# Hybrid S5 and differential-attention layer: the low-k pass of the scores as two matmuls on 64 rows

## The chip, the cores and the metric

The kernel runs on one core of one Trainium2 chip. The metric is device time in microseconds (us), the median of several executions. One further execution was taken by the hardware profiler; the rows below come from it.

## The reference, cut to what matters

One encoder layer is applied to two requests, a prompt of 256 tokens and a sample of 1024 tokens. Beside the attention it has a state-space branch, gates and projections, which the change leaves alone. The part in question:

```python
q = _rotary(q.reshape(Bsz, L, N_HEADS, 2, HEAD_DIM))   # 4 heads, 2 streams, 64 channels
k = _rotary(k.reshape(Bsz, L, N_HEADS, 2, HEAD_DIM))
def block(qi):                                         # 128 queries at a time
    s = jnp.einsum('bqhtd,bkhtd->bthqk', qi, k).astype(jnp.float32) * scale
    p = jax.nn.softmax(s, axis=-1)
    w = p[:, 0] - lam * p[:, 1]
    return jnp.einsum('bhqk,bkhe->bqhe', w, v)
```

## The kernel before, in words

The kernel works at float32 accuracy with a faster matmul type: every operand is split into a high part and a low part (suffixes h and l), and a product is the sum of high·high, high·low and low·high.

The attention stage goes head by head (4 heads). A head has five pairs of query blocks: four pairs over the 1024 sample tokens (pi 0 to 3, the long units) and one over the 256 prompt tokens (pi 4, the short units). A unit is one block of 128 queries (qi). `unit_scores` computes, for each of the two streams t, a score tile S of 128 queries by nk keys (two banks of 512 float32 columns for a long unit). Its contraction has only 64 channels, so q's tile holds the high part in partitions 0 to 63 and the low part in 64 to 127, and the k tile holds the same 64 channels twice. One matmul on 128 rows with k's high part (line 924) thus gives high·high plus low·high. A second one with k's low part (line 926) gives high·low plus low·low. For each t of a long unit that is four matmuls of 512 columns: two at line 924, two at line 926.

Behind the scores VectorE (DVE) takes the row maximum (line 928), ScalarE (ACT) the exponential (line 932), GpSimd (POOL) and VectorE combine the two streams (lines 939, 940). TensorE (PE) transposes the weights (line 949) and multiplies them with v (lines 961 to 963). Between these stand "filler" steps (lines 706 to 708), gate projections that are independent of the attention and are interleaved by counts (`F_LONG`, `F_SHORT`). A static scheduler fixes each engine's order when the program is built.

`load_head` loads a head's operands from DRAM on SyncE's (SP's) DMA queue into buffers shared with the earlier stage. In the rows the tags are: hU (q of t=0, and v's high part), htb (k's high part of t=0, and q of t=1), hmt (k's low part of t=0, and v's low part), hwcm (k's high part of t=1, and the short units' parts), hwb (k's low part of t=1). All tags have two buffers, hwb has one.

Two other places of the program use only a part of the array and are read below: line 440, in the preparation of the state-space matrices, with 32 columns of the array (shape "128*32"), and lines 275 and 276 with 32 of its rows ("32*128").

Of the kernel before, what the change touches and what calls it, by code (L numbers as in the profile page):

```python
# [11 lines left out]
F32 = mybir.dt.float32  # L12
# [10 lines left out]
LL = 1024  # L23
LS = 256
NT = LL + LS
# [101 lines left out]
def kernel(  # L127
# [6 lines left out]
    V, G, A, PE, SP = nc.vector, nc.gpsimd, nc.scalar, nc.tensor, nc.sync  # L134
# [3 lines left out]
    def dram(shape, dtype, name):  # L138
        return tc.dram_tile(shape, dtype, name=name)
# [7 lines left out]
    q_d = [dram([2, 2, 128, NT], F32, f"q_d{i}") for i in range(2)]  # L147
    k_d = [dram([2, 2, 128, NT], F32, f"k_d{i}") for i in range(2)]
# [572 lines left out]
    def fill(steps, ins=None):  # L721
        with after(ins):
            for _ in range(steps):
                next(filler, None)
# [4 lines left out]
    with ExitStack() as p2:  # L729
# [20 lines left out]
        def load_wb(b):  # L750
            wb = (sp_ if b % 2 else sl).tile([128, 2, NB, 128], F32, tag="wb", name="wb")
            SP.dma_start(wb, wb_d[b])
            return wb
# [81 lines left out]
        with tc.manual_schedule(engines={mybir.EngineType.PE, mybir.EngineType.SP}):  # L835
# [10 lines left out]
            for b in range(NBLK):  # L846
                q = b // 2
# [22 lines left out]
    with ExitStack() as p3:  # L870
# [5 lines left out]
        def load_head(h):  # L876
            pr, cb = h // 2, (h % 2) * 2
            big = lambda tag, b: sl.tile([128, NT], F32R, tag=tag, name=f"h{tag}", bufs=b)
            sml = lambda tag, b: sl.tile([128, LL], F32R, tag=tag, name=f"h{tag}", bufs=b)
            q0, k00, q1, vh = big("U", 2), big("tb", 2), big("tb", 2), big("U", 2)  # L880
            k10, k01, k11, vl, rest = sml("mt", 2), sml("wcm", 2), sml("wb", 1), sml("mt", 2), sml("wcm", 2)
            part = lambda i: rest[:, i * LS:(i + 1) * LS]
            v3 = lambda t: t.rearrange("p (k e) -> p k e", e=128)

            def load_q(t, q):
                rows = slice((cb + t) * 32, (cb + t) * 32 + 32)
                for s in range(2):
                    for f in range(2):
                        o = s * 64 + f * 32
                        SP.dma_start(q[o:o + 32].bitcast(F32), q_d[pr][s, f, rows])  # L890

            def load_k(t, hl, k, c0, n):
                rows = slice((cb + t) * 32, (cb + t) * 32 + 32)
                for s in range(2):
                    for f in range(2):
                        o = s * 64 + f * 32
                        SP.dma_start(k[o:o + 32].bitcast(F32), k_d[pr][hl, f, rows, c0:c0 + n])

            load_q(0, q0)
            load_k(0, 0, k00, 0, NT)  # L900
            load_k(0, 1, k10, 0, LL)
            load_q(1, q1)
            load_k(1, 0, k01, 0, LL)
            load_k(1, 1, k11, 0, LL)
            SP.dma_start(v3(vh).bitcast(F32), vh_d[h])
            SP.dma_start(v3(vl).bitcast(F32), vl_d[h][:, 0:8])
            load_k(0, 1, part(0), LL, LS)
            load_k(1, 0, part(1), LL, LS)
            load_k(1, 1, part(2), LL, LS)
            SP.dma_start(v3(part(3)).bitcast(F32), vl_d[h][:, 8:10])  # L910
            return (([q0[:, :LL], q1[:, :LL]], [k00[:, :LL], k01], [k10, k11], v3(vh)[:, 0:8], v3(vl)),
                    ([q0[:, LL:], q1[:, LL:]], [k00[:, LL:], part(1)], [part(0), part(2)],
                     v3(vh)[:, 8:10], v3(part(3))))

        def unit_scores(hd, qi, nk, fu):
            qs, kh, kl = hd[:3]
            pt = []
            sm = ap.tile([128, 2], F32, tag="sm", name="sm", bufs=2)
            for t in range(2):
                S = ps_s.tile([128, LL], F32, tag=f"S{t}", name=f"S{t}")  # L920
                qw = qs[t][:, qi * 128:qi * 128 + 128]
                cks = [(c, min(512, nk - c)) for c in range(0, nk, 512)]
                for c, n in cks:
                    PE.matmul(S[:, c:c + n], qw, kh[t][:, c:c + n], start=True, stop=False)  # L924
                for c, n in cks:
                    last = PE.matmul(S[:, c:c + n], qw, kl[t][:, c:c + n], start=False, stop=True)  # L926
                mx = ap.tile([128, 1], F32, tag=f"mx{t}", name=f"mx{t}", bufs=2)
                V.tensor_reduce(mx, S[:, :nk], axis=AX.X, op=ALU.max)  # L928
                V.tensor_scalar(mx, mx, -1.0 / math.sqrt(HD), None, op0=ALU.mult)  # L929
                p = ap.tile([128, LL], F32, tag=f"p{t}", name=f"p{t}", bufs=3 - t)  # L930
                with tc.issue_after(tables.ins):
                    A.activation(p[:, :nk], S[:, :nk], AF.Exp, bias=mx, scale=1.0 / math.sqrt(HD),  # L932
                                 accum_out=sm[:, t:t + 1])
                pt.append(p)
                fill(fu[t], last if fu[t] else None)
            rs = ap.tile([128, 2], F32, tag="rs", name="rs", bufs=2)
            V.reciprocal(rs, sm)  # L937
            V.tensor_tensor(rs[:, 1:2], rs[:, 1:2], nlam, op=ALU.mult)
            G.tensor_scalar(pt[0][:, :nk], pt[0][:, :nk], rs[:, 0:1], 1.0, op0=ALU.mult, op1=ALU.mult)  # L939
            V.scalar_tensor_tensor(pt[0][:, :nk], pt[1][:, :nk], rs[:, 1:2], pt[0][:, :nk], op0=ALU.mult, op1=ALU.add)  # L940
            return pt[0]
# [71 lines left out]
        for h in range(NH):  # L1013
            parts = load_head(h)
            for pi in range(5):
                nk = LL if pi < 4 else LS
                fl = F_LONG if pi < 4 else F_SHORT
                hd = parts[pi // 4]
                wTh = ap.tile([128, 8, 256], F32R, tag="wTh", name="wTh", bufs=2)
                wTl = ap.tile([128, 8, 256], F32R, tag="wTl", name="wTl", bufs=2)  # L1020
                for qi in range(2):
                    w = unit_scores(hd, (pi % 4) * 2 + qi, nk, fl)
                    if prev:
                        finish(prev, fl[2])
                    else:
                        fill(fl[2])
                    fill(fl[3])
                    prev = (h, pi, qi, w, hd, wTh, wTl)
# [21 lines left out]
    def split_into(h, l, src):  # L1050
        ins = A.copy(h, src)
        V.tensor_tensor(l, src, h, op=ALU.subtract)
        return ins
# [98 lines left out]
    for grp in range(2):  # L1152
# [4 lines left out]
        wb = load_wb(0)  # L1157
        for f in range(8):
            bh, bl = wb
            if f < 7:  # L1160
                wb = load_wb(f + 1)
# [13 lines left out]
            last = split_into(mh[:, f], ml[:, f], s1)  # L1175
# [75 lines left out]
```

## Time and profile before

| | us |
|---|---|
| median of 3 runs | 1127.63 (1127.1 to 1129.29) |
| the profiled execution's own time | 1127.2 |
| its span | 1125.1 |
| TensorE busy (matmul) | 1067.2 |
| TensorE busy (weight load) | 987.1 |
| VectorE busy | 801.0 |
| ScalarE busy | 462.5 |
| GpSimd busy | 354.8 |

The span is the time from the first to the last recorded instruction. "PE" is the matmul row of TensorE, "PEld" its weight loads, which overlap the matmuls. Matmuls are pipelined: one is recorded longer than the distance to the next, so that distances between starts say what a stream of them costs. A row of the timeline may merge neighbours of one line ("x2"); its time then runs from the first one's start to the last one's end.

### The profile page before, as it was taken

How to read it: one execution, taken by the hardware profiler on the slowest of the kernel's cores; microseconds unless marked ns; L12 is line 12 of the kernel's file. 1: busy time of each engine (PE TensorE's matmuls, PEld its weight loads, DVE VectorE, ACT ScalarE, POOL GpSimd, SP SyncE). 2: the span in 40 equal slices, each digit the busy share in tenths (PEclk: the TensorE clock that was granted, in tenths of full speed). 3: DMA queues.
4: the chain of work that ended last, by engine and by line, in shares of the span. 5: the costliest groups of instructions: out<-in, count | busy, mean ns of one | idle time of the engine just before them, and what ended most of it. 6: DMA issues, size and time to landing. Idle time of an engine off the chain costs nothing.

```text
span 1125.1 us, 18000 instructions
## 1 busy us (share of the span) xinstructions
PE 1067.2 (95%) x6479; PEld 987.1 (88%) x6479; DVE 801.0 (71%) x1533; ACT 462.5 (41%) x927; POOL 354.8 (32%) x437
## 2 busy tenths in 40 slices
PE   5999799999989999999999999999999999998997
PEld 4878588788979988898999998989999999998997
DVE  5998997888579999478677777766442675666524
ACT  4453222332312121455555645554453445544332
POOL 2447999511032333122122222212141003520032
PEclk9999899999999999999999999999999999999999
DMA  7745453654596676615416316311645975569112
GB/s 212 170 141 188 142 174 117 209 166 156 173 282 174 205 202 168 177 51 150 141 47 169 122 47 186 114 40 60 210 124 174 292 230 128 167 194 270 48 57 94
DMA packets 186154, 173.59 MB, mean 154 GB/s; under 512 B 32721, under 2 KB 161745, under 8 KB 186066
## 3 DMA queue, kind: packets, MB, share of 16 engines
q1 hardware_dynamic: 150738, 144.13, 43.6%
q10 hardware_dynamic: 35328, 28.32, 7.9%
q8 instruction: 51, 0.84, 0.3%
q14 instruction: 37, 0.30, 0.1%
HBM read 113.71 MB, written 58.69 MB: 153 GB/s over the span
## 4 chain that ended last, share of the span: by engine, by line
PE 47%; DVE 18%; DMA 7%; ACT 4%; issue 3%; POOL 2%; SPq 0%; ACTq 0%; POOLq 0%; DVEq 0%
PE mm L706 5%; PE mm L707 5%; PE mm L708 5%; PE xb L1058 3%; PE xb L1059 3%; PE xb L1060 3%; PE pb L246 2%; PE pb L248 2%; PE pb L247 2%; DVE z L797 2%; DVE z L798 2%; PE S L924 2%; DMA yt<-ya_d 2%; PE S L926 2%; DVE mx L928 2%
## 5 line engine op out<-in xcount | busy, mean ns | idle before, releaser
L706 PE MATMUL mm<-hTh,wh 128*128 128x424 f32 (+1 forms) x576 | 212.2, 368 | 6.3 <-ACT zo L712 6.3
L708 PE MATMUL mm<-hTh,wl 128*128 128x424 f32 (+1 forms) x576 | 206.1, 358 | 0.0
L707 PE MATMUL mm<-hTl,wh 128*128 128x424 f32 (+1 forms) x576 | 206.0, 358 | 0.0
L706 PEld LDWEIGHTS mm<-hTh,wh 128*128 128x128 f32 x576 | 109.2, 190 | 12.6 <-ACT zo L712 8.1
L707 PEld LDWEIGHTS mm<-hTl,wh 128*128 128x128 f32 x576 | 109.2, 190 | 4.6
L708 PEld LDWEIGHTS mm<-hTh,wl 128*128 128x128 f32 x576 | 109.0, 189 | 3.4
L928 DVE TENSOR_REDUCE mx<-S 128x1 f32<-128x1024 f32 (+1 forms) x80 | 84.2, 1057 | 38.9 <-PE S L926 38.7
L939 POOL TENSOR_SCALAR p<-p,rs 128x1024 f32<-128x1024 f32 (+1 forms) x40 | 41.7, 1042 | 205.0 <-DVE rs L937 194.2
L246 PE MATMUL pb<-hTh,wh 128*128 128x512 f32 (+1 forms) x288 | 105.7, 367 | 0.0
L247 PE MATMUL pb<-hTl,wh 128*128 128x512 f32 (+1 forms) x288 | 105.1, 365 | 0.0
L932 ACT ACTIVATE p<-S,mx 128x1024 f32<-128x1024 f32 (+1 forms) x80 | 79.2, 992 | 63.0 <-DVE mx L929 53.8
L248 PE MATMUL pb<-hTh,wl 128*128 128x512 f32 (+1 forms) x288 | 103.9, 361 | 0.4 <-DVE wl L240 0.4
L240 POOL TENSOR_TENSOR wl<-wst,wh 128x1024 fp32r<-128x1024 f32 x24 | 64.3, 2679 | 126.5 <-ACT wh L239 51.7
L1191 PE MATMUL tr<-wqh,mh 128*128 128x256 f32 x320 | 89.7, 280 | 1.5 <-DVE o L1195 1.3
L1192 PE MATMUL tr<-wql,mh 128*128 128x256 f32 x320 | 89.3, 279 | 0.0
L1193 PE MATMUL tr<-wqh,ml 128*128 128x256 f32 x320 | 89.0, 279 | 0.0
L248 PEld LDWEIGHTS pb<-hTh,wl 128*128 128x128 f32 x288 | 54.6, 190 | 9.3 <-DVE wl L240 0.9
L246 PEld LDWEIGHTS pb<-hTh,wh 128*128 128x128 f32 x288 | 54.7, 190 | 8.6
L1191 PEld LDWEIGHTS tr<-wqh,mh 128*128 128x128 f32 x320 | 60.1, 188 | 2.4 <-DVE o L1195 2.4
L247 PEld LDWEIGHTS pb<-hTl,wh 128*128 128x128 f32 x288 | 54.6, 190 | 8.4
L1198 POOL TENSOR_TENSOR o<-o,finB 128x256 f32<-128x256 f32 x30 | 27.9, 934 | 103.8 <-ACT jk L1197 103.8
L1192 PEld LDWEIGHTS tr<-wql,mh 128*128 128x128 f32 x320 | 60.1, 188 | 0.0
(387 smaller groups left out, 2793.4 us busy)
## 6 DMA issues: line engine op xcount, KB each, us to landing
wst<-in_w_in_dram ACTq DMA_DIRECT2D x24, 512.0 KB, 4.0
wst<-in_w_in_dram SPq DMA_DIRECT2D x16, 512.0 KB, 4.8
wst<-in_w_branch_dram SPq DMA_DIRECT2D x32, 256.0 KB, 4.4
wqs<-in_w_out_dram SPq DMA_DIRECT2D x16, 512.0 KB, 3.8
tt_d<-tt SPq DMA_DIRECT2D x16, 320.0 KB, 2.6
tb<-tt_d SPq DMA_DIRECT2D x8, 640.0 KB, 5.1
zt<-gs_d SPq DMA_DIRECT2D x16, 320.0 KB, 4.3
x<-in_x_sample_dram SPq DMA_DIRECT2D x8, 512.0 KB, 4.6
```

Of the source, the lines that this page charges most:

```text
L240: e.tensor_tensor(lv, st, hv, op=ALU.subtract)
L246: PE.matmul(ps[:, :n], wh[:, k, :], hTh[:, k, c0:c0 + n], start=(k == 0), stop=False)
L247: PE.matmul(ps[:, :n], wh[:, k, :], hTl[:, k, c0:c0 + n], start=False, stop=False)
L248: PE.matmul(ps[:, :n], wl[:, k, :], hTh[:, k, c0:c0 + n], start=False, stop=(k == KD - 1))
L706: PE.matmul(ps[:, :n], wh[:, k, :], hTh[:, k, c0:c0 + n], start=(k == 0), stop=False)
L707: PE.matmul(ps[:, :n], wh[:, k, :], hTl[:, k, c0:c0 + n], start=False, stop=False)
L708: PE.matmul(ps[:, :n], wl[:, k, :], hTh[:, k, c0:c0 + n], start=False, stop=(k == KD - 1))
L928: V.tensor_reduce(mx, S[:, :nk], axis=AX.X, op=ALU.max)
L932: A.activation(p[:, :nk], S[:, :nk], AF.Exp, bias=mx, scale=1.0 / math.sqrt(HD), accum_out=sm[:, t:t + 1])
L1191: PE.matmul(ps[:, :256], mh[:, k, ts_], oh_[:, k], start=(k == 0), stop=False)
L1192: PE.matmul(ps[:, :256], mh[:, k, ts_], ol_[:, k], start=False, stop=False)
L1193: PE.matmul(ps[:, :256], ml[:, k, ts_], oh_[:, k], start=False, stop=(k == 7))
```

## The change

The high-k pass (line 924 before, 936 after) stays as it is. The low-k pass of the long units no longer takes q's low part along, so the product low·low is left out. The pass has two matmuls on 64 rows: key chunk 0 with q's high part in partitions 0 to 63, key chunk 1 with q's high part in partitions 64 to 127. The one writes the first bank of S, the other the second. For that, q's high part must lie in both halves: q of t=0 keeps high above low, q of t=1 is loaded with low above high, and a new tile qx (in hwb's buffer) holds the missing halves. The low parts of k for both t now share one tile klo (an hmt buffer), 512 columns for each t. Short units keep the old form.

```diff
-            def load_q(t, q):
+            def load_q(t, q, o, hl, n=NT):
                 rows = slice((cb + t) * 32, (cb + t) * 32 + 32)
-                for s in range(2):
-                    for f in range(2):
-                        o = s * 64 + f * 32
-                        SP.dma_start(q[o:o + 32].bitcast(F32), q_d[pr][s, f, rows])
+                for f in range(2):
+                    SP.dma_start(q[o + f * 32:o + f * 32 + 32].bitcast(F32), q_d[pr][hl, f, rows, 0:n])
...
+            def load_klo(t):
+                rows = slice((cb + t) * 32, (cb + t) * 32 + 32)
+                for s in range(2):
+                    for f in range(2):
+                        o = s * 64 + f * 32
+                        SP.dma_start(klo[o:o + 32, t * 512:t * 512 + 512].bitcast(F32),
+                                     k_d[pr][1, f, rows, s * 512:s * 512 + 512])
+
+            load_q(0, q0, 0, 0)
+            load_q(0, q0, 64, 1)
             load_k(0, 0, k00, 0, NT)
-            load_k(0, 1, k10, 0, LL)
-            load_q(1, q1)
+            load_klo(0)
+            load_q(0, qx, 64, 0, LL)
+            load_q(1, q1, 64, 0)
+            load_q(1, q1, 0, 1)
             load_k(1, 0, k01, 0, LL)
-            load_k(1, 1, k11, 0, LL)
+            load_klo(1)
+            load_q(1, qx, 0, 0, LL)
...
+            his = ((q0[0:64], qx[64:128]), (qx[0:64], q1[64:128]))
+            los = [[(his[t][s], klo[64 * s:64 * s + 64, t * 512:t * 512 + 512]) for s in range(2)] for t in range(2)]
...
-                for c, n in cks:
-                    last = PE.matmul(S[:, c:c + n], qw, kl[t][:, c:c + n], start=False, stop=True)
+                if nk == LL:
+                    for (c, n), (qh_, kl_) in zip(cks, kl[t]):
+                        last = PE.matmul(S[:, c:c + n], qh_[:, qi * 128:qi * 128 + 128], kl_, start=False, stop=True)
+                else:
+                    last = PE.matmul(S[:, :nk], qw, kl[t], start=False, stop=True)
```

TensorE's order at the first unit of the first head, before (S is the score tile, mm a filler's bank):

```order
L708 MATMUL mm<-hTh,wl 128x424
L924 MATMUL S_5018<-htb,hU 128x512 x2
L926 MATMUL S_5018<-hmt,hU 128x512 x2
L706 MATMUL mm<-hTh,wh 128x432
L707 MATMUL mm<-hTl,wh 128x432
```

The same place of the changed kernel:

```order
L708 MATMUL mm<-hTh,wl 128x424
L936 MATMUL S_5022<-htb,hU 128x512 x2
L939 MATMUL S_5022<-hmt,hU 128x512
L939 MATMUL S_5022<-hmt,hwb 128x512
L706 MATMUL mm<-hTh,wh 128x432
L707 MATMUL mm<-hTl,wh 128x432
```

Only the operands of the second pair differ; the number of matmuls and every place in TensorE's order are the same, and so are the orders of VectorE, ScalarE and GpSimd in the whole program.

SyncE's DMA queue at the change from the first head to the second, before:

```order
L897 DMA hmt<-k_d_91 32x1024 x4
L897 DMA hwcm<-k_d_91 32x1024 x4
L897 DMA hwb<-k_d_91 32x1024 x4
L997 DMA ya_d_95<-ya 128x512
L897 DMA htb<-k_d_91 32x1280
L890 DMA hU<-q_d_89 32x1280 x4
```

And in the changed kernel:

```order
L895 DMA hwcm<-k_d_91 32x1024
L902 DMA hmt<-k_d_91 32x512 x4
L888 DMA hwb<-q_d_89 32x1024 x2
L895 DMA hwcm<-k_d_91 32x1024 x3
L902 DMA hmt<-k_d_91 32x512 x4
L1012 DMA ya_d_95<-ya 128x512
L888 DMA hwb<-q_d_89 32x1024 x2
L895 DMA htb<-k_d_91 32x1280
L888 DMA hU<-q_d_89 32x1280 x4
```

Four more issues per head, of the same bytes in all, stand ahead of the load of the next head's htb; two of them behind the store of ya.

## Rows read from the trace of the kernel before

**Rows 1.** Windows of the whole attention stage and of one stretch; PEclk is granted clock.

```profile
core 0: us, PE busy (x) PEld busy (x) DVE busy (x) ACT busy (x) POOL busy (x), PEclk, DMA share, GB/s
457.00:775.00 318.00, 309.24 (x1804) 287.00 (x1804) 232.66 (x420) 171.05 (x347) 72.77 (x51) 0.99 0.37 109
470.00:475.00 5.00, 4.42 (x17) 3.90 (x18) 1.41 (x3) 0.55 (x3) 0.00 (x0) 0.66 0.25 81
```

**Rows 2.** Waits of PE in that stage: us in total, times, longest.

```profile
PE S L924 <- ACT p L932: 5.8, 6, 2.1
PE tr L949 <- DVE wTl L953: 1.4, 2, 0.7
PE tr L949 <- DVE mx L929: 1.3, 3, 0.5
```

**Rows 3.** PE timeline of the first unit: start us, us, instruction.

```profile
457.41 0.36 PE L708 MATMUL mm<-hTh,wl 128*128 128x424 f32 x1
457.61 0.63 PE L924 MATMUL S<-htb,hU 128*128 128x512 f32 x2
458.07 0.62 PE L926 MATMUL S<-hmt,hU 128*128 128x512 f32 x2
458.53 0.36 PE L706 MATMUL mm<-hTh,wh 128*128 128x432 f32 x1
```

**Rows 4.** Line 926, matmuls on long units: ns min/median/max, first and last start.

```profile
L926 PE MATMUL S<-hmt,hU x64: 387/396/628, 458.1 to 759.5; 128*128 128x512 f32 x64
L926 PE MATMUL S<-hwb,htb x64: 387/394/403, 461.3 to 762.8; 128*128 128x512 f32 x64
```

**Rows 5.** PE timeline around one group of line 440.

```profile
150.03 0.28 PE L247 MATMUL pb<-hTl,wh 128*128 128x256 f32 x1
150.14 0.28 PE L248 MATMUL pb<-hTh,wl 128*128 128x256 f32 x1
150.35 0.25 PE L440 MATMUL tr<-Cr,Bb 128*32 128x16 f32 x4
...
150.48 0.18 PE L440 MATMUL tr<-Cna,Bb 128*32 128x16 f32 x1
150.59 0.48 PE L443 MATMUL tr<-wc,Bm 128*128 128x256 f32 x1
```

**Rows 6.** Weight loads of the same group.

```profile
150.03 0.19 PEld L248 LDWEIGHTS pb<-hTh,wl 128*128 128x128 f32 x1
150.35 0.15 PEld L440 LDWEIGHTS tr<-Cr,Bb 128*32 128x32 f32 x4
150.41 0.11 PEld L440 LDWEIGHTS tr<-Cna,Bb 128*32 128x32 f32 x1
150.59 0.19 PEld L443 LDWEIGHTS tr<-wc,Bm 128*128 128x128 f32 x1
```

**Rows 7.** PE and weight-load timelines at lines 547 and 275 (32 rows).

```profile
29.17 0.28 PE L547 MATMUL mm<-Wvh,hTl 128*128 128x256 f32 x1
29.38 0.24 PE L275 MATMUL tr<-ident,an 32*128 32x32 f32 x1
29.37 0.13 PEld L275 LDWEIGHTS tr<-ident,an 32*128 32x128 f32 x1
```

**Rows 8.** PE timeline where the type changes, the shape of the array not.

```profile
184.43 0.39 PE L246 MATMUL pb<-hTh,wh 128*128 128x512 f32 x1
184.66 0.27 PE L418 MATMUL tr<-ident,wbp 128*128 128x128 f32 x1
```

**Rows 9.** PE timeline at a score pair whose weight load nothing hid.

```profile
513.20 0.74 PE L924 MATMUL S<-htb,hU 128*128 128x512 f32 x2
```

**Rows 10.** SyncE's DMA issues at the change of heads, and PE at the next head.

```profile
514.45 1.70 SPq L897 DMA_DIRECT2D hmt<-k_d  x4
516.24 1.77 SPq L897 DMA_DIRECT2D hwcm<-k_d  x4
518.11 1.81 SPq L897 DMA_DIRECT2D hwb<-k_d  x4
524.32 0.34 SPq L997 DMA_DIRECT2D ya_d<-ya  x1
526.82 0.30 SPq L897 DMA_DIRECT2D htb<-k_d  x1
...
529.02 1.35 SPq L897 DMA_DIRECT2D htb<-k_d  x3
...
537.49 0.64 PE L924 MATMUL S<-htb,hU 128*128 128x512 f32 x2
```

**Rows 11.** DMA issues: KB each, median us from issue to landing.

```profile
htb<-k_d SPq DMA_DIRECT2D x16, 160.0 KB, 4.0
```

More of the change, by code (lines that the diff above doesn't have):

```diff
@@ L880, in load_head @@
             q0, k00, q1, vh = big("U", 2), big("tb", 2), big("tb", 2), big("U", 2)
-            k10, k01, k11, vl, rest = sml("mt", 2), sml("wcm", 2), sml("wb", 1), sml("mt", 2), sml("wcm", 2)
+            klo, k01, qx, vl, rest = sml("mt", 2), sml("wcm", 2), sml("wb", 1), sml("mt", 2), sml("wcm", 2)
             part = lambda i: rest[:, i * LS:(i + 1) * LS]
             v3 = lambda t: t.rearrange("p (k e) -> p k e", e=128)
-            def load_q(t, q):
+            def load_q(t, q, o, hl, n=NT):
                 rows = slice((cb + t) * 32, (cb + t) * 32 + 32)
-                for s in range(2):
-                    for f in range(2):
-                        o = s * 64 + f * 32
-                        SP.dma_start(q[o:o + 32].bitcast(F32), q_d[pr][s, f, rows])
+                for f in range(2):
+                    SP.dma_start(q[o + f * 32:o + f * 32 + 32].bitcast(F32), q_d[pr][hl, f, rows, 0:n])
             def load_k(t, hl, k, c0, n):
@@ L897, in load_k @@
                         SP.dma_start(k[o:o + 32].bitcast(F32), k_d[pr][hl, f, rows, c0:c0 + n])
-            load_q(0, q0)
+            def load_klo(t):
[7 more added lines that the diff above has]
+            load_q(0, q0, 64, 1)
             load_k(0, 0, k00, 0, NT)
-            load_k(0, 1, k10, 0, LL)
-            load_q(1, q1)
+            load_klo(0)
+            load_q(0, qx, 64, 0, LL)
+            load_q(1, q1, 64, 0)
+            load_q(1, q1, 0, 1)
             load_k(1, 0, k01, 0, LL)
-            load_k(1, 1, k11, 0, LL)
+            load_klo(1)
+            load_q(1, qx, 0, 0, LL)
             SP.dma_start(v3(vh).bitcast(F32), vh_d[h])
@@ L910, in load_head @@
             SP.dma_start(v3(part(3)).bitcast(F32), vl_d[h][:, 8:10])
-            return (([q0[:, :LL], q1[:, :LL]], [k00[:, :LL], k01], [k10, k11], v3(vh)[:, 0:8], v3(vl)),
+            his = ((q0[0:64], qx[64:128]), (qx[0:64], q1[64:128]))
+            los = [[(his[t][s], klo[64 * s:64 * s + 64, t * 512:t * 512 + 512]) for s in range(2)] for t in range(2)]
+            return (([q0[:, :LL], q1[:, :LL]], [k00[:, :LL], k01], los, v3(vh)[:, 0:8], v3(vl)),
                     ([q0[:, LL:], q1[:, LL:]], [k00[:, LL:], part(1)], [part(0), part(2)],
```

## The prediction

> **What bounds the kernel now.** I read the windows first, because the change touches one stage only. Over the attention stage, 318 us long, TensorE's matmul row is busy for 309 us, VectorE for 233 and ScalarE for 171, at a granted clock of 0.99, so at the 2.4 GHz level nearly throughout [rows 1]. Then the waits: TensorE stood still there for 5.8 + 1.4 + 1.3 = 8.5 us in 11 places [rows 2]. So TensorE bounds this stage, and with the order of every compute engine unchanged, what a score pair costs or saves on TensorE lengthens or shortens the whole, less what goes into those 8.5 us.
>
> Busy time does not tell what a matmul costs, since records overlap. The distance between starts does: two matmuls of 512 columns take 458.07 − 457.61 = 0.46 us, the next two 458.53 − 458.07 = 0.46, so one costs 0.23 [rows 3]. One of 256 columns costs 150.14 − 150.03 = 0.11 to 0.12 us [rows 5]. Column count sets the cost; the weight load, 0.19 us on record, runs under the matmul before it and starts with it (150.03 in both rows) [rows 5, 6].
>
> The two rows of line 926 hold 128 matmuls of 512 columns [rows 4]. They become 64 pairs of matmuls on 64 rows each.
>
> **What a pair saves.** If the two halves of the array run side by side, the pair costs one matmul instead of two. No row shows two 64-row matmuls. The nearest rows are those of line 440, small matmuls that use two different column groups of the array: four weight loads stand within 0.15 us though one takes 0.11, so they start about 0.01 us apart and run together, and seven matmuls start within 150.48 − 150.35 = 0.13 us [rows 5, 6]. I take side by side, offset 0.01: the pair saves 0.23 − 0.01 = 0.22 us. The other bound is nothing saved.
>
> **What the switch costs.** Before the pair the array works as 128 by 128, in it as two tiles of 64 rows, behind it as 128 by 128 again. Line 440 shows such a change of shape in both directions.
>
> Going in: the last full matmul starts at 150.14, and the next weight load only at 150.35, 0.21 us later instead of at once [rows 5, 6]. In a stream of 256 columns the next matmul would have started after 0.12, so the load waits 0.09 us past the hand-over. Lines 547 and 275 show the same with 32 rows in place of 32 columns: 29.37 − 29.17 = 0.20 [rows 7]. So it isn't peculiar to column groups. It isn't the change of type either: from line 246 to line 418 the type changes and the array's shape doesn't, and the starts are 0.23 apart, as in a stream of 512 columns [rows 8].
>
> A load that can't run under the matmul before it is then exposed. Its price is in a score pair that followed a wait: 0.74 us for two matmuls where the first unit's took 0.63, so 0.11 us [rows 3, 9]. Going in costs 0.09 + 0.11 = 0.20 us.
>
> Coming out: the last matmul of line 440 has only 16 columns and starts at 150.48; the full-size load behind it starts at 150.59 [rows 5, 6]. That is 0.11 us, of which the columns themselves are under 0.01 at 0.23 us per 512. So the load waits some 0.10 us beyond the stream, and then 0.11 us lie open: 0.21, less the 0.01 by which a normal hand-over exceeds the stream (twice 256 columns at 0.11 against 0.23). Coming out costs 0.20 us.
>
> The Trainium skill, in "TensorEngine Tiling (Array Packing)", section Key Properties, says that changing the tiling mode, as against only the tile, drains the engine; it gives no price. The rows agree at 32 columns and at 32 rows; none shows 64 rows.
>
> **The sum.** A pair costs 0.20 + 0.20 − 0.22 = +0.18 us, and 64 pairs +11.5 us. The bounds of a switch that the rows do not show for 64 rows are 0 (then −0.22 a pair, −14.1 us) and 0.40 as read.
>
> TensorE's waits take some of it back. Where TensorE now waits for ScalarE's exponential or VectorE, it arrives later by the bubbles that lie between; 11 waits by about 0.2 us is 2.2, but some stand in the short units, which hold no pair. I take 1.5 us off, between 0 and 4. VectorE isn't delayed by the pair itself: the pair ends 0.20 + 0.01 − 0.23 = −0.02 us against before, and the cost behind it falls on the next filler or transpose.
>
> **The DMA queue** I cost at nothing. At the first change of heads three sets of loads go out from 514.45, 516.24 and 518.11 [rows 10]. Now klo's buffer comes free only with the last long pair, where hwb's did, at 518.1. From there 13 issues (4 klo, 2 qx, 3 hwcm, 4 klo) follow at 1.81 / 4 = 0.45 us, to about 524.0. The store of ya, which they stand ahead of, went out at 524.32, so it waits no longer than before. Two more issues behind it end near 525.6, and htb couldn't go before 526.82, when the short unit freed it [rows 10]. The cover is 0.3 us there and 1.2 here. If it is gone, htb is late by as much; but its last piece, issued at about 530 and landing 4.0 us later, is read at 537.49, with 3 us to spare [rows 10, 11]. The first head's loads go out in the stage before.
>
> So the profiled execution's 1127.2 us becomes 1127.2 + 11.5 − 1.5 = 1137.2. The median shown is 0.4 above that execution, hence 1137.6 us. The change makes the kernel slower by 0.9%.
>
> **Rivals.** First, **no bubble at 64 rows**: the loads of the halves slip in under the running full matmul, and the full load under the pair. Then each pair saves 0.22 us, 14.1 us in all; the waits grow by some 1.5 us, since TensorE then reaches ScalarE's results earlier, which leaves 1127.6 − 12.6 = 1115 us. It decides if the bubbles of both sides together are under 0.22 us. For it speaks that the traces show no 64-row tile; against it, that two different shapes both show the wait going in. The Trainium skill, in "TensorE: Matmul & The Clock Gate", section Measured speedup vs the span model, gives a pack of row tiles one matmul's time and about 4 ns per further tile; it knows no price for entering, so by it this case would come out. The rows bear out the running together, but not an entry that is free. Chance 0.13.
>
> Second, **only one side pays**: the one exit that the rows price stands behind a 16-column matmul, which leaves no time to load under; behind 512 columns the full load may find room in the background. Then a pair costs 0.20 − 0.22 = −0.02, 64 pairs −1.3 us: 1126.3 us, no measurable change. Against it: in the stream of 256 columns going in, there was time enough and the load still waited. Chance 0.08.
>
> Third, **the halves' weight loads queue**: the second starts when the first is through, 0.11 us later instead of 0.01. That adds 0.10 a pair, 6.4 us: 1144 us. Line 440's loads run together, but in different columns, not rows. Chance 0.12.
>
> Fourth, **the halves run in turn**, and the change doesn't do what it says: +0.22 more a pair, 14.1 us, 1151.7 us. Chance 0.05.
>
> **Numbers.** My forecast has 0.62; its own range is 1132 to 1142: the two prices of 0.20 are read from rows with hundredths and two decimals, so ±0.04 a pair or ±2.6 us, and 0 to 4 us go into waits. One fall of the clock to its lower level, 1.2 GHz, as in the stretch from 470 to 475 (granted 0.66, about a third of 5 us lost [rows 1]), adds 1.7 us; more idle gaps on TensorE could bring one or two. The whole range reaches from the one-sided case, 1125, to the queued loads with a fall of the clock, 1146, and leaves out the first and the fourth rival, together 0.18. A change of this kernel's time can be told from none at about 0.2%, 2.3 us. Slower: 0.62 + 0.12 + 0.05 = 0.79. Same: 0.08. Faster: 0.13.
>
> **What would show it.** In the changed profile, at a long unit's line 939: the first load of the pair 0.09 us past the normal hand-over, that is some 0.3 us after the start of the last 512-column matmul of line 936, and not under it; two matmuls of 512 columns that start within 0.02 us; the next full load some 0.3 us after the second one's start. From the start of the second matmul of line 936 to the first filler behind the pair it should be about 0.87 us, where it is now 3 × 0.23 = 0.69. The attention stage should be about 10 us longer, the stages around it as before, TensorE's waits shorter, the granted clock near 0.99. I am wrong if the loads of line 939 start with the matmul before them, if the pair's second matmul starts 0.1 us or more after the first, or if a wait for htb or hwb appears at the change of heads.

## The result, and the profile after

The changed kernel took 1134.83 us (median of 10 runs, 1129.94 to 1140.92), the kernel before 1127.22 in 10 runs beside it. The ratio is 1.0056, with a 95% interval of 1.004 to 1.0073: slower by 6.3 us, between 4.5 and 8.2 (the two medians by themselves stand 7.6 apart). The forecast was 1137.6. The profiled execution took 1134.15 us with a span of 1132.1.

The window of the attention stage, now ten microseconds longer to hold the whole of it, and TensorE's waits in it:

```profile
core 0: us, PE busy (x) PEld busy (x) DVE busy (x) ACT busy (x) POOL busy (x), PEclk, DMA share, GB/s
457.00:785.00 328.00, 322.75 (x1838) 275.22 (x1837) 234.98 (x426) 174.83 (x353) 73.19 (x52) 1.00 0.36 108
```

```profile
PE S L936 <- ACT p L947: 3.5, 6, 0.9
PE tr L964 <- DVE wTl L968: 1.4, 2, 0.7
```

The waits fell from 8.5 us [rows 2] to 3.5 + 1.4 = 4.9. The granted clock is 1.00 in the whole window, the 2.4 GHz level; the dip of the kernel before [rows 1] isn't there. Ahead of that dip TensorE had stood still for 2.1 us, the longest wait of [rows 2]; at the same place of the changed kernel it stood still for 0.28. How much the stage grew is read from the starts of the high-k pass at its ends, which the view of one source line gives for line 924 before and 936 after. Before:

```profile
L924 PE MATMUL S<-htb,hU x72: 277/396/504, 457.6 to 772.1; 128*128 128x512 f32 x64, 128*128 128x256 f32 x8
L924 PE MATMUL S<-hwcm,htb x72: 277/396/497, 460.9 to 773.8; 128*128 128x512 f32 x64, 128*128 128x256 f32 x8
```

After:

```profile
L936 PE MATMUL S<-htb,hU x72: 276/397/501, 459.4 to 777.9; 128*128 128x512 f32 x64, 128*128 128x256 f32 x8
L936 PE MATMUL S<-hwcm,htb x72: 278/396/504, 462.8 to 779.4; 128*128 128x512 f32 x64, 128*128 128x256 f32 x8
```

That is 773.8 − 457.6 = 316.2 us before and 779.4 − 459.4 = 320.0 after. The two are not at one clock: the dip cost the kernel before some 1.7 us of its 316.2, by the prediction's own reckoning. The experiment e1 gives the comparison without it. Outside the stage the two spans differ by 3.2 us (1132.1 − 320.0 against 1125.1 − 316.2), which is within the spread of single executions.

Now one pair in the stream, on TensorE's timeline, and its weight loads below. It answers to [rows 3].

```profile
500.85 0.35 PE L708 MATMUL mm<-hTh,wl 128*128 128x424 f32 x1
501.04 0.63 PE L936 MATMUL S<-hwcm,htb 128*128 128x512 f32 x2
501.59 0.49 PE L939 MATMUL S<-hmt,hwb 64*128 64x512 f32 x1
501.60 0.49 PE L939 MATMUL S<-hmt,htb 64*128 64x512 f32 x1
502.02 0.46 PE L706 MATMUL mm<-hTh,wh 128*128 128x424 f32 x1
502.32 0.36 PE L707 MATMUL mm<-hTl,wh 128*128 128x424 f32 x1
```

```profile
500.85 0.38 PEld L936 LDWEIGHTS S<-hwcm,htb 128*128 128x128 f32 x2
501.59 0.18 PEld L939 LDWEIGHTS S<-hmt,hwb 64*128 64x128 f32 x1 [0.36 <-issue]
501.60 0.18 PEld L939 LDWEIGHTS S<-hmt,htb 64*128 64x128 f32 x1
502.02 0.19 PEld L706 LDWEIGHTS mm<-hTh,wh 128*128 128x128 f32 x1 [0.24 <-issue]
```

The reader is to see five things. The loads of line 936 stand at 500.85, under the filler ahead of their matmuls. The second matmul of line 936 began at 501.27 (the two end at 501.67, and one of them is recorded with 0.40). The pair's first load comes only at 501.59, 0.32 to 0.33 later instead of at once: 0.10 beyond the hand-over after 0.23. The two halves start within 0.01 of each other. And the next full load waits until 502.02, 0.42 behind the second half.

The exposed loads show as longer records: 0.49 for a half (line 936: 0.40), 0.46 for the filler behind it (its neighbours 0.35 and 0.36), so 0.10 on each side. It is so for every half, as the view of line 939 shows (ns, smallest, median, largest): no record is under 491.

```profile
L939 PE MATMUL S<-hmt,hwb x64: 491/492/502, 459.9 to 768.5; 64*128 64x512 f32 x64
L939 PE MATMUL S<-hmt,hU x32: 491/493/500, 459.9 to 765.0; 64*128 64x512 f32 x32
L939 PE MATMUL S<-hmt,htb x32: 491/498/502, 463.4 to 768.5; 64*128 64x512 f32 x32
```

From the second matmul of line 936 to the filler's stream: 0.33 + 0.42 + 0.11 = 0.86 us, where three matmuls of 0.23 took 0.69. A pair costs +0.17 us (0.168 before rounding), 64 pairs 10.8 us.

One pair of the 64 doesn't stand side by side. In its place TensorE's order, before as after, has ten matmuls of the weights with v between the two low-k matmuls, so that each half makes a visit of its own, at 0.39 us more than the same matmul takes in e1:

```profile
651.12 0.49 PE L939 MATMUL S<-hmt,hwb 64*128 64x512 f32 x1
652.91 0.50 PE L939 MATMUL S<-hmt,htb 64*128 64x512 f32 x1
```

The time grew by 6.3. The experiments ask whether that price is right, and where the rest went.

### The profile page after: what moved, and what is told of

Its sections match the earlier page's. It is cut to its first block, busy times and chain, and to the rows that moved or that the text cites. A ratio compares the mean times of both kernels' runs of the same rounds, so it can differ in the third digit from the quotient of the medians.

```text
span 1132.1 us, 18014 instructions
## 1 busy us (share of the span) xinstructions
PE 1078.1 (95%) x6479; PEld 971.7 (86%) x6479; DVE 800.1 (71%) x1533; ACT 463.1 (41%) x927; POOL 355.4 (31%) x437
## 4 chain that ended last, share of the span: by engine, by line
PE 43%; DVE 20%; DMA 8%; issue 3%; ACT 3%; POOL 2%; SPq 1%; ACTq 0%; POOLq 0%; DVEq 0%
PE mm L706 5%; PE mm L707 5%; PE mm L708 5%; DVE z L798 3%; DVE z L797 3%; PE pb L246 2%; PE xb L1073 2%; PE pb L247 2%; PE pb L248 2%; PE xb L1074 2%; PE xb L1075 2%; PE S L936 2%; PE tr L964 2%; DVE mx L943 2%; PE tr L1206 2%
## 5 line engine op out<-in xcount | busy, mean ns | idle before, releaser
L706 PE MATMUL mm<-hTh,wh 128*128 128x424 f32 (+1 forms) x576 | 216.4, 376 | 5.5 <-ACT zo L712 5.5
L706 PEld LDWEIGHTS mm<-hTh,wh 128*128 128x128 f32 x576 | 108.7, 189 | 20.3 <-issue 10.2
```

The lines of the kernel that those rows point to most:

```text
L706: PE.matmul(ps[:, :n], wh[:, k, :], hTh[:, k, c0:c0 + n], start=(k == 0), stop=False)
```

## The experiments

The theory was that entering and leaving the 64-row shape costs 0.39 to 0.40 us for each visit, that each pair saves 0.23 by running side by side, and that TensorE's waits take some of the difference back. The rivals were that the new loads and buffers cost the time, and that the price lies with the pair itself and not with the visit.

**e1_loads_only** has the loads, buffers and tiles of the changed kernel, but its low-k pass runs on all 128 rows. Half of its low-k matmuls take other operands than the product asks for; what they cost is the same.

```diff
-                    for (c, n), (qh_, kl_) in zip(cks, kl[t]):
-                        last = PE.matmul(S[:, c:c + n], qh_[:, qi * 128:qi * 128 + 128], kl_, start=False, stop=True)
+                    for i, (c, n) in enumerate(cks):
+                        w_ = qw if i == t else kl[2][:, qi * 128:qi * 128 + 128]
+                        last = PE.matmul(S[:, c:c + n], w_, kl[t], start=False, stop=True)
```

> The changed kernel's loads and tiles, with the low-k pass as two matmuls on all 128 rows (the scores' low part is then a wrong sum; the work is that of before). The order of every compute engine is that of before. Theory (each visit to the 64-row shape costs TensorE about 0.39 us, the loads nothing): as before, 1127 us, within 0.2%. Rival (the loads of qx and klo, or the longer hold on their buffers, cost what was measured): 1133 to 1135 us.

Measured: 1126.48 us (12 runs) against 1127.21, ratio 0.9996 (0.9981 to 1.0011). The loads cost nothing that can be measured, that is, not more than 1.2 us by the interval, and the slowdown is on TensorE's side. TensorE's waits in its stage are nearly those of the kernel before:

```profile
PE S L935 <- ACT p L947: 4.8, 6, 1.2
PE tr L964 <- DVE wTl L968: 1.4, 2, 0.7
PE tr L964 <- DVE mx L944: 1.3, 3, 0.5
```

Its stage has no dip of the clock either (granted 1.00), so it is the one to set the changed kernel's 320.0 us against:

```profile
L935 PE MATMUL S<-htb,hU x72: 277/396/500, 458.3 to 770.4; 128*128 128x512 f32 x64, 128*128 128x256 f32 x8
L935 PE MATMUL S<-hwcm,htb x72: 277/396/507, 461.6 to 772.0; 128*128 128x512 f32 x64, 128*128 128x256 f32 x8
```

That is 772.0 − 458.3 = 313.7 us; between these two executions the pairs make the stage 6.3 us longer.

**e2_in_turn** puts both low-k matmuls of a pair on the same 64 rows, so that they can't run side by side; qx and its loads fall away.

```diff
-            his = ((q0[0:64], qx[64:128]), (qx[0:64], q1[64:128]))
-            los = [[(his[t][s], klo[64 * s:64 * s + 64, t * 512:t * 512 + 512]) for s in range(2)] for t in range(2)]
+            his = (q0[0:64], q1[64:128])
+            los = [[(his[t], klo[64 * t:64 * t + 64, s * 512:s * 512 + 512]) for s in range(2)] for t in range(2)]
```

> Both low-k matmuls of a stream on the same 64 rows (t=0 the upper half, t=1 the lower), so that they can't run side by side; no qx, fewer loads. Order of all compute engines as before. Theory (side by side saves 0.23 us a pair, the visit costs 0.39): 64 x 0.39 = 25 us over before less 2 to 5 that go into waits, 1147 to 1150 us. Rival (the two halves never ran side by side in the changed kernel, their records only start together): as the changed kernel, 1134 us.

Measured: 1144.2 us (4 runs), ratio 1.0147 (1.0124 to 1.0169), 16.6 us slower than before (14.0 to 19.1), less than the 1147 to 1150 expected and far above the rival's 1134. One visit on its timeline:

```profile
458.42 0.61 PE L932 MATMUL S<-htb,hU 128*128 128x512 f32 x2
458.96 0.73 PE L935 MATMUL S<-hmt,hU 64*128 64x512 f32 x2
459.62 0.46 PE L706 MATMUL mm<-hTh,wh 128*128 128x432 f32 x1
```

The switch is the same as in the changed kernel: the second matmul of line 932 began at 458.42 + 0.61 − 0.40 = 458.63, the pair 0.33 behind it, and the filler's record has 0.46. From the start of the pair to the next full load it takes 459.62 − 458.96 = 0.66, where side by side took 0.42 to 0.43. So side by side saves 0.23, and the whole difference to 128 rows is 0.17 + 0.23 = 0.40 a visit, 25.7 us for 64. Measured were 16.6: here, too, less than the price, and here the waits are shorter still:

```profile
PE S L932 <- ACT p L943: 1.7, 3, 0.6
PE tr L960 <- DVE wTl L964: 1.4, 2, 0.7
```

The waits alone can't be the whole of that difference: 25.7 − 16.6 = 9.1 us is more than the 8.5 of waits that there were, and 3.1 are left. The section on the prediction takes it apart.

**e6_order_alone** and **e3_one_visit** put two pairs into one visit. For that, the scores of both streams stand together: first the four high-k matmuls, then the four low-k ones. e6 does this alone, on 128 rows; e3 has the same order on every engine, and the streams side by side on 64 rows each. So e3 against e6 tells the cost of the visit without that of the order.

```diff
             for t in range(2):
...
-                for c, n in cks:
-                    last = PE.matmul(S[:, c:c + n], qw, kl[t][:, c:c + n], start=False, stop=True)
+            if nk == LL:
+                for i, (c, n) in enumerate(cks):
+                    lasts = []
+                    for t in range(2):
+                        qh_, kl_ = kl[t][i]
+                        with tc.issue_after(last.ins):
+                            last = PE.matmul(Ss[t][:, c:c + n], qh_[:, qi * 128:qi * 128 + 128], kl_, start=False, stop=True)
+                        lasts.append(last)
```

> The kernel before with the order of the kernel above: high-k passes of both streams, then the low-k passes on 128 rows. Nothing is left out. If VectorE and ScalarE follow as now, 1127 us; if the later first maximum opens waits on TensorE, up to 1132 us.

> One visit per unit instead of two: the high-k pass of both streams first, then t=0 in the upper half beside t=1 in the lower half, for key chunk 0 and then 1; no qx. To be read against the next kernel, which has the same order. Theory (the price is per visit): 32 visits x 0.39 less 64 x 0.23 saved, so 2 us under the next kernel. Rival (the price is per pair of 64-row matmuls): 64 pairs x 0.17, 6 to 11 us over it. How the order itself does is open: a wait for both score tiles at once may add up to 5 us to both.

Measured: e6 1143.66 us (5 runs), ratio 1.014 (1.0119 to 1.0161); e3 1144.04 us (5 runs), ratio 1.0144 (1.0122 to 1.0166). The order alone costs 16 us, where I had expected 5 at most. TensorE's waits have grown most where it waits for ScalarE's exponential, in 20 places instead of 6. All its waits in the stage come to 17.2 us, 8.7 more than before, so about half of the 16; where the rest arises was not followed up. The two largest:

```profile
PE S L926 <- ACT p L944: 9.1, 20, 0.9
PE tr L961 <- DVE mx L941: 3.4, 5, 0.9
```

A visit with two pairs, in e3:

```profile
459.17 0.67 PE L934 MATMUL S<-hwcm,htb 128*128 128x512 f32 x2
459.77 0.49 PE L943 MATMUL S<-hmt,hU 64*128 64x512 f32 x1
459.77 0.50 PE L943 MATMUL S<-hmt,htb 64*128 64x512 f32 x1
460.10 0.39 PE L943 MATMUL S<-hmt,hU 64*128 64x512 f32 x1
460.11 0.39 PE L943 MATMUL S<-hmt,htb 64*128 64x512 f32 x1
460.43 0.47 PE L706 MATMUL mm<-hTh,wh 128*128 128x432 f32 x1
```

Only the first pair has records of 0.49 to 0.50; the second, loaded under the first, has 0.39. The switch is paid for once. From the last full matmul to the filler's stream it is 0.33 + 0.34 + 0.32 + 0.11 = 1.10 us, against 5 × 0.23 = 1.15 on 128 rows: 0.05 us a unit gained, some 1.6 us in 32 units. The difference measured between e3 and e6, 0.4 us with some 3.4 either way, cannot tell 1.6 from none, but it excludes a price per pair of 0.17, which would give 10.8, and also the 6.3 that came through in the changed kernel.

**e8_order_fill, e7_one_visit_fill, e9_before_fill, e10_after_fill** move fillers from behind the attention stage into it, so that TensorE has fewer waits and every microsecond of its work counts. e8 is e6, and e7 is e3, with two more filler steps in each long unit; e9 is the kernel before, and e10 the changed kernel, with one more. e7 and e8 have the same orders on all engines, and so have e9 and e10.

```diff
-F_LONG = (4, 1, 2, 0)
+F_LONG = (4, 3, 2, 0)
```

```diff
-F_LONG = (4, 1, 2, 0)
+F_LONG = (4, 2, 2, 0)
```

> The order of e6 (scores of both streams one after the other, all passes on 128 rows) with two more filler steps ahead of each long unit's scores (F_LONG 4, 3, 2, 0); the fillers come out of the tail behind the attention. Theory: e6 lost its 16 us to TensorE's waits for ScalarE's exponential (9.1 us in 20 places) and its like; with more filler these go, so 1128 to 1136 us. Rival: the order costs elsewhere, and it stays at 1140 or above.

> One visit to 64 rows per long unit with two pairs side by side, with the same engine orders as e8. Where TensorE's time counts in full: theory (a price of 0.39 us for each visit, 0.23 saved by each pair, so 0.39 - 2 x 0.23 = -0.07 us a unit, 32 units): 2 us faster than e8. Rival, the switch is paid for by each pair: +0.17 x 64 = 11 us slower than e8. If e8 is freed of its waits, this kernel may come under the kernel before, at 1125 to 1128 us.

> The kernel before with one more filler step ahead of each long unit's scores (F_LONG 4, 2, 2, 0), all passes on 128 rows. The fillers come out of the tail, so TensorE's work is the same; what may go are its 8.5 us of waits in the stage. Theory: 1119 to 1126 us, the waits are largely gone. Rival: the waits move, 1127 us or more.

> The changed kernel with the same one more filler step, with the same engine orders as e9. Theory: the visits cost 0.168 us for each of 64 pairs, 10.8 us, and the changed kernel showed only 6.3 of it because TensorE's waits took the rest; with fewer waits left to take it, it should be 8 to 11 us above e9. Rival: the price of a pair is the smaller one (6.3 / 64 = 0.10 us), and the distance to e9 stays at 6 or below.

Measured, against 1129.06 us of the kernel before: e8 1170.4 us, ratio 1.0368 (1.0347 to 1.0388); e7 1170.13, ratio 1.0363 (1.0345 to 1.0381); e9 1134.12, ratio 1.005 (1.003 to 1.007); e10 1146.56, ratio 1.0159 (1.0134 to 1.0184).

As times of their own the four are misses: none is faster, and I had expected e8 at 1136 at most and e9 at 1126 at most. In e8 TensorE now waits behind the attention, at line 1070, for the attention's result:

```profile
PE xb L1070 <- ACT yah L1063: 23.1, 4, 12.5
```

The fillers that I moved had hidden that. In e9 the waits for ScalarE did go (5.8 to 0.4 us), but others came, at the changes of heads:

```profile
PE S L924 <- DMA htb<-q_d: 5.3, 2, 4.0
PE S L924 <- ACT p L932: 0.4, 1, 0.4
```

As pairs they tell what they were made for. e10 has nearly the same waits as e9, with the smaller ones that are left out here 8.2 us in its stage against 7.4:

```profile
PE S L936 <- DMA hwb<-q_d: 5.3, 1, 5.3
PE S L936 <- DMA htb<-q_d: 1.7, 1, 1.7
```

In both it is mostly DMA that TensorE waits for, and the pairs did not shorten that. The stage, from the view of the high-k line, of e9 and of e10:

```profile
L924 PE MATMUL S<-htb,hU x72: 276/393/767, 457.9 to 788.5; 128*128 128x512 f32 x64, 128*128 128x256 f32 x8
L924 PE MATMUL S<-hwcm,htb x72: 278/393/487, 461.1 to 790.6; 128*128 128x512 f32 x64, 128*128 128x256 f32 x8
```

```profile
L936 PE MATMUL S<-htb,hU x72: 274/397/767, 458.5 to 800.1; 128*128 128x512 f32 x64, 128*128 128x256 f32 x8
L936 PE MATMUL S<-hwcm,htb x72: 278/396/504, 461.9 to 802.2; 128*128 128x512 f32 x64, 128*128 128x256 f32 x8
```

That is 790.6 − 457.9 = 332.7 and 802.2 − 458.5 = 343.7: 11.0 us more, 10.2 without the 0.8 of waits. The clock differs, too. In both it fell behind the longest of these waits (4.0 us in e9, 5.3 in e10). The seven microseconds from the end of that wait, of e9 and of e10 (columns as in the window above):

```profile
533.46:540.46 7.00, 7.00 (x27) 6.22 (x28) 2.60 (x6) 0.59 (x1) 0.48 (x1) 0.64 0.24 68
537.84:544.84 7.00, 7.00 (x30) 5.69 (x31) 2.60 (x6) 1.09 (x3) 0.48 (x1) 0.75 0.37 102
```

TensorE is busy throughout, and the granted 0.64 and 0.75 take 0.36 × 7 = 2.5 us of it in e9 and 0.25 × 7 = 1.75 in e10. With these 0.8 us set right the difference is 11.0 again, where the price read from the pair gives 10.8. (In this order two pairs have their halves apart, which adds to the price.) By the ratios e10 is 1.0159 / 1.005 = 1.0108 of e9, 12 us, and with the two intervals added in quadrature, 9 to 16. So where the waits take nothing, the pairs cost nearly what they cost on the timeline. The rival, a smaller price of 0.10 a pair, falls. e7 against e8 is −0.3 us, again not to be told from −2, and not +11.

No version came under the kernel before by what can be measured. A visit with two pairs would gain at most some 2 us, and every order tried that allows one lost more.

## Why the prediction was right, and which term was mis-sized

**TensorE bounds the stage**: right. Its busy time is 322.75 of 328 us, and what it does longer lengthens the stage. e1 shows that nothing else in the change does, within 1.2 us.

**Going in, 0.20 us**: 0.10 of waiting and 0.10 of exposed load, 0.19 or 0.20 as read. The rows with 32 columns and with 32 rows [rows 5 to 7] told it for 64 rows.

**Coming out, 0.20**: 0.42 from start to load, less 0.10 of the pair's own exposed load and 0.23 of columns, leaves 0.09 to 0.10 of waiting; the filler's load adds 0.11. Right where a filler stands behind the pair, and so the stream of 512 columns gave no room to load under: the one-sided rival falls. One of the signs was written down wrongly: the full load was to come 0.3 us behind the second start and came at 0.42, because the record of the half begins with its exposed load. The distance over all, 0.87 us, was right (0.86).

**Side by side, 0.22**: the halves start within 0.01, and e2 shows what it is worth, 0.23. The Trainium skill, in "TensorE: Matmul & The Clock Gate", section Measured speedup vs the span model, gives about 4 ns between tiles. The trace agrees: 3 to 4 ns lie between the starts of the halves in the 63 pairs. The rivals of halves that queue or run in turn fall. So does the rival without a bubble: the pairs show 0.10 us of waiting on each side. The Trainium skill, in "TensorEngine Tiling (Array Packing)", section Key Properties, says that a change of the tiling mode drains the engine; the waiting on both sides agrees with it.

**The DMA queue at nothing**: right, though not at the times that were worked out. SyncE's timeline of the changed kernel, answering to [rows 10]:

```profile
515.62 1.72 SPq L902 DMA_DIRECT2D hmt<-k_d  x4
519.71 2.22 SPq L902 DMA_DIRECT2D hmt<-k_d  x4
524.43 0.34 SPq L1012 DMA_DIRECT2D ya_d<-ya  x1
524.82 0.90 SPq L888 DMA_DIRECT2D hwb<-q_d  x2
527.07 0.30 SPq L895 DMA_DIRECT2D htb<-k_d  x1
```

The thirteen issues began at 515.62 and not at 518.1, so klo's buffer came free earlier than reckoned, and they were through at 521.9 instead of 524.0; the store went out at 524.43 and htb at 527.07, where they stood at 524.32 and 526.82. No wait for htb or hwb appears. In e10 one for hwb does, of 5.3 us: the term was nothing in this order, not in any.

**Taken back by the waits, 1.5 us (0 to 4)**: this term of the sum was mis-sized, and the price of the pairs a little. The traces show by how much. Between the first and the last start of the high-k pass, the traces of e1 and of the changed kernel hold the same 1792 matmuls in the same order, both at a granted clock of 1.00, so that every distance between two starts can be compared with its counterpart. At the pairs (from the matmul ahead of a pair to the second one behind it) the distances grow by 10.1 us in sum, where 11.5 were forecast: the 41 pairs with a filler behind them cost 0.165 on the average, ten with a transpose behind them only 0.115, the one whose halves stand apart 0.78; the other twelve differ among themselves. Everywhere else the distances shrink by 3.7 us, 3.1 of them in eleven places, most of them waits of e1. That leaves the 6.3 by which the stage grew (10.07 − 3.73 before rounding). For e2 against e1 the same sum gives 24.0 us at the visits and 5.4 taken back, 18.6 in the stage, which its time (14.0 to 19.1) allows.

So about 3.7 us were taken back where 1.5 had been set. The working had multiplied 11 waits by one bubble of 0.2. The first wait in the stage shows that one can take in more. Two units, and so four pairs (0.67 us), lie ahead of it. In e1:

```profile
470.34 0.50 PE L935 MATMUL S<-htb,hU 128*128 128x512 f32 x1 [1.16 <-ACT p L947]
```

and in the changed kernel:

```profile
471.14 0.74 PE L936 MATMUL S<-htb,hU 128*128 128x512 f32 x2 [0.28 <-ACT p L947]
```

It lost 0.88 us, where one bubble of 0.2 had been reckoned; the four pairs can account for 0.67 of it. The size of this wait differs between executions (2.1 in [rows 2]), and how many bubbles each wait takes in was not tried by itself: that they take in several is a reading of the traces. e2 agrees in direction: with more than twice the price, 5.4 us were taken back instead of 3.7.

With 10.1 and 3.7 in place of 11.5 and 1.5 the sum would have been 1127.6 + 10.1 − 3.7 = 1134.0 us; 1134.83 was measured, inside the range of 1125 to 1146 and inside the likeliest case's own, 1132 to 1142.

One thing the prediction had left out: a fall of the clock could only add time in it, while the profile that it started from held one already, of 1.7 us. The changed kernel's profiled execution has none in this stage. How often it comes in the executions that were not profiled isn't known.

## What to carry to other kernels

Price a change of the array's shape by the visit and not by the matmul: here one visit cost 0.39 us, and two 512-column matmuls side by side gave back 0.23, so that a visit with one pair lost and one with two pairs about broke even. Look for the price in any stretch of the same profile where the shape changes already. And when TensorE's own work grows in a stage where it sometimes waits, reckon that a wait may take in the additions of several units ahead of it, look whether the clock is the same on both sides before subtracting two windows, and find out what the fillers hide before moving them.

## What the runs showed of the hardware that was not expected

That the weight loads of the second pair of a visit do run under the first pair (records of 0.39 against 0.49 in e3), though those of the first don't run under a full matmul, nor the full load under the pair. And that two half loads are recorded with 0.18 us each and cost 0.10 together when nothing hides them, as much as one full load (0.19 recorded, 0.11 exposed).
